# A streaming encoder step on one Trainium2 core: sample attention with its components combined ahead of the transposes, split V, and split squares in the norm

## Chip, cores and metric

The kernel runs on one core of one Trainium2 chip. The metric is the device time of one execution in microseconds (us). Before the change it is the median of three runs. A profile of one further execution gives the spans of the engines: TensorE (PE), VectorE (DVE), ScalarE (ACT), GpSimd (POOL), and SyncE (SP), which issues every DMA of this kernel.

## The reference

One layer of a hybrid encoder, for a new stream of 2048 frames (the prompt) and for 64 next frames of a running stream (the sample) that has 4096 past frames. Everything is fp32. Cut to what matters here:

```python
def diff_attention(q, k, v, q_pos, k_pos, lam, slopes):     # 4 heads, 2 components c of 64, values of 128
    s = jnp.einsum('bqhcd,bkhcd->bhcqk', q, k).astype(jnp.float32) * (DK_A ** -0.5)
    dist = jnp.abs(q_pos[:, None] - k_pos[None, :]).astype(jnp.float32)
    s = s - slopes[None, :, None, None, None] * dist[None, None, None]
    allowed = (k_pos[None, :] // CHUNK) <= (q_pos[:, None] // CHUNK)
    s = jnp.where(allowed[None, None, None], s, -jnp.inf)
    p = jax.nn.softmax(s, axis=-1)
    a = p[:, :, 0] - lam * p[:, :, 1]
    return jnp.einsum('bhqk,bkhe->bqhe', a.astype(v.dtype), v)

def layer_output(x, oa, ob, za, zb, ga, gb, subln_g, lam_init, w_oa, w_ob, w_out):
    oa = (rmsnorm(oa, subln_g) * (1.0 - lam_init)).reshape(B, T, W_A) * jax.nn.silu(za)
    ob = rmsnorm(ob).reshape(B, T, W_B) * jax.nn.silu(zb)
    m = ga * (oa @ w_oa) + gb * (ob @ w_ob)
    return x + m @ w_out
...
        h = rmsnorm(x, norm_g) @ w_in      # 6144 columns: q, k, v, z of attention and retention, gates
        k_all = jnp.concatenate([cache_k_diff[l].astype(ka.dtype), ka], axis=1)
        v_all = jnp.concatenate([cache_v_diff[l].astype(va.dtype), va], axis=1)
        oa = diff_attn_step(qa, k_all, v_all, past, lam, slopes)
```

The sample's attention is thus 64 queries against 4096 + 64 keys in 4 heads with 2 components. The second branch (retention, per chunk of 64 frames) is computed beside it.

## The kernel before, in words

**Order.** The instruction order of PE, ACT and DVE is written out by a planner inside the kernel. Each piece of work is a Python generator with a priority. The planner keeps a model clock for each engine (`P`, `A`, `V`, `G`, lines 119 to 133; `ld` for DMAs, which are modelled as bytes at 300 per ns plus 2600 ns). At each step `loop` runs the generator of best priority whose wake time has come on PE's model clock; a generator yields the time at which its next input should be there. Buffers are counted with `take` and `give`. On the chip every engine runs its instructions in that order and waits on semaphores; SP's DMA queue is in order too.

**Streams.** The w stream (priority 9, the last) multiplies the normalised x with w_in, in two halves of 1024 frames, the first with the sample's 64 frames. Its matmuls are L500; operands are split into a high and a low fp32r part, three products each. Weights are loaded into three staging buffers ("ws"), cast by ACT (L462), subtracted by POOL (L472), and kept in twelve buffers. Results are taken out of PSUM (tag "mm", two buffers) by ACT (L770) or by the finishing routines, and stored to scratch in DRAM. The z stream (priority 4) runs, half by half, the prompt's attention (`qk_block`, `softmax`, `at_pv`), in the first half also the sample's attention and retention, and the prompt's retention (`ret_block`, matmuls L1301 and on). The second half's attention waits until the w stream has made that half's q, k and v. When both streams have ended, the out stream (L1556 on) applies the output projections.

**Sample attention** (`sample_attn`, L1080). Queries of both components stand on the 128 rows: component 0 in rows 0..63, component 1 in rows 64..127. For a head, eight blocks of 512 cached keys and one of 64 new ones are loaded (`s_loader`, tag K), split into two fp32r parts (ACT L1146, DVE L1148), multiplied (L1111 to L1113), and taken out with the position bias by DVE (L1121) into four row buffers of 128 x 1024 and a tail of 64. ACT exponentiates (L1168, L1173) and sums. `sample_pv` (L1209) then runs in nine steps: four transposes (L1242) of 128 x 128, a copy out of PSUM by ACT (L1256) or DVE (L1253) into "ath" or "atl", and four fp32 matmuls (L1228) with P as the stationary and V as the moving operand, 128 columns. Rows of both components go through the transposes and the matmuls. The result is scaled by row with 1/sum or -lambda/sum (L1266), and after four heads a matmul with `fold` (L1181) adds the two row halves.

**Norm of the attention output** (`rms_t`, L794). With the features on the partitions, the mean of squares is a matmul of a constant 1/128 matrix with the squares. It runs 32 times for the prompt (4 heads, 8 pairs of blocks) and once for the sample:

```python
        nc.scalar.activation(sq, ps, AF.Square)
        t1 = self.A(n, t)
        nc.scalar.copy(o, ps)
        t2 = self.A(n, t)
        self.give(tag, t2)
        yield t1
        yield from self.take("tp")
        mb = self.psum("tp")[:, :n]
        nc.tensor.matmul(mb, self.ones, sq, start=True, stop=True)
```

**Buffers.** `ROWS` = 8 row buffers of 4 KB a partition; K and V have four buffers each.

Of the kernel before, what the change touches and what calls it, by code (L numbers as in the profile page):

```python
# [60 lines left out]
class Hybrid:  # L61
# [732 lines left out]
    def rms_t(self, ps, n, gain, t, tag, tmp=None):  # L794
        nc = self.nc
        if tmp is None:
            for k in ("r_o", "r_sq", "r_y"):
                yield from self.take(k)
            tmp = [self.sb(self.tp_, [128, 256], k)[:, :n] for k in ("r_o", "r_sq", "r_y")]
            own = True  # L800
        else:
            own = False
        o, sq, y = tmp
        nc.scalar.activation(sq, ps, AF.Square)
# [7 lines left out]
        nc.tensor.matmul(mb, self.ones, sq, start=True, stop=True)  # L812
# [9 lines left out]
        nc.vector.scalar_tensor_tensor(out=sq, in0=mb, scalar=EPS, in1=sq, op0=ALU.add, op1=ALU.mult)  # L822
# [257 lines left out]
    def sample_attn(self):  # L1080
        nc = self.nc
# [8 lines left out]
        for h in range(4):  # L1090
# [84 lines left out]
            self.spawn(self.sample_pv(h, units, tail, te, lp, oall), 2, "z")  # L1175
        yield lambda: self.n_spv == 4
# [12 lines left out]

    def s_loader(self):  # L1190
        for h in range(4):
            for m in range(8):
# [15 lines left out]

    def sample_pv(self, h, units, tail, te, lp, oall):  # L1209
        nc = self.nc  # L1210
        ap, sp = self.ap, self.sp
        yield te[-1]
        w = sp.tile([128, 1], F32, tag="s_w", name="s_w", bufs=3)
        nc.vector.tensor_reduce(w, lp[:, :9], axis=AX.X, op=ALU.add)
        nc.vector.reciprocal(w, w)
        nc.vector.tensor_mul(w, w, self.lsam)
        for _ in range(3):
            tw = self.V(9)
        yield from self.take("pv")
        pv = self.psum("pv")[:, :128]  # L1220
        done = [0.0]

        def mms(m, nt, r, a, tag, t):
            yield lambda: len(self.vcs) > 0
            vc, t2 = self.vcs.pop(0)
            yield max(t, t2)
            for k in range(nt):
                nc.tensor.matmul(pv, a[:r, 128 * k:128 * k + 128], vc[:r, k, :],  # L1228
                                 start=m == 0 and k == 0, stop=m == 8)
                done[0] = self.P(512)  # L1230
            self.give(tag, done[0])
            self.give("V", done[0])
            yield self.pe

        todo = None
        for m in range(9):
            nt, r = (4, 128) if m < 8 else (1, 64)
            yield from self.take("at")
            at = self.psum("at")
            for k in range(nt):  # L1240
                src = units[m // 2][:, (m % 2) * 512 + 128 * k:(m % 2) * 512 + 128 * k + 128] if m < 8 else tail
                nc.tensor.transpose(at[:r, 128 * k:128 * k + 128], src, self.ident)  # L1242
                t = self.P(256)
            if m < 8 and m % 2:
                self.give("row", t)
            tag = ("ath", "atl")[m % 2]
            if todo is not None and not self.has(tag):
                yield from mms(*todo)
                todo = None
            yield from self.take(tag)  # L1250
            a = self.sb(ap, [128, 512], tag, "atp")
            if m % 2:
                nc.vector.tensor_copy(a[:r, :128 * nt], at[:r, :128 * nt])  # L1253
                t = self.V(128 * nt, t)
            else:
                nc.scalar.copy(a[:r, :128 * nt], at[:r, :128 * nt])  # L1256
                t = self.A(128 * nt, t)
            self.give("at", t)
            yield self.pe
            if todo is not None:  # L1260
                yield from mms(*todo)
            todo = (m, nt, r, a, tag, t)
# [4 lines left out]
        self.t_spv = self.V(128, max(t, tw))  # L1267
        self.give("pv", self.t_spv)
        self.n_spv += 1
# [8 lines left out]
    def ret_block(self, k, t0, r, first):  # L1278
# [477 lines left out]
    def run(self):  # L1756
# [19 lines left out]
        with tc.manual_schedule(engines=MANUAL(ET)):  # L1776
            self.ident = self.cp.tile([128, 128], F32, tag="ident", name="ident")
            self.xt_ready = []
            self.ones = self.cp.tile([128, 128], F32, tag="ones", name="ones")
            nc.vector.memset(self.ones, 1.0 / 128.0)  # L1780
# [76 lines left out]
```

## Time and profile before

| | |
|---|---|
| runs shown | 2001.48 us median (2001.47 to 2004.52, three runs) |
| the profiled execution | 2002.83 us |
| its span, first to last instruction | 2001.0 us |
| granted TensorE clock, mean | 0.999 |
| sample QK matmuls (L1111) | 421.7 to 572.5 us |
| sample PV matmuls (L1228) | 460.3 to 595.9 us, 264 instructions |
| norm's matmuls (L812) | 219.8 to 1511.8 us, 66 instructions |

How to read the rows quoted below: an engine's busy time is the union of its instructions' spans. Matmuls are pipelined and their ends are modelled, so the length of one matmul is longer than the distance to the next; where a price is wanted, the distance of starts is used. "PEld" is the weight load, which overlaps matmuls. A row of a group has: line, engine, operation, written tile <- read tiles, shape, xcount, and durations min/median/max in ns or busy us and mean ns. A row of waits has: who waits <- for whom, us in total, times, longest. An fp32 matmul appears as two instructions in the counts, a transpose or an fp32r matmul as one. A row of "busy tenths" divides the span into 40 slices of 50 us.

### The profile page before, as it was taken

What the parts mean: (1) busy time and instruction counts of PE and PEld (TensorE: products, weight loads), DVE (VectorE), ACT (ScalarE), POOL (GpSimd) and SP (SyncE); (2) the same over time, 40 slices, a digit from 0 to 9 for tenths busy, and PEclk for the clock granted to TensorE, in tenths of its full rate; (3) what the DMA queues carried; (4) which work ended last, traced back from release to release, by engine and by line L of the source; (5) the groups of instructions that cost most, each with busy time, mean ns of one, the idle gap of its engine ahead of it and who ended that gap; (6) DMA issues with size and microseconds to landing.
All of it is one profiled execution on the core that took longest, in us unless ns stands there. A gap on an engine that the chain in (4) does not pass through costs nothing.

```text
span 2001.0 us, 34243 instructions
## 1 busy us (share of the span) xinstructions
PE 1985.4 (99%) x12402; PEld 1780.0 (89%) x12402; DVE 992.0 (50%) x2665; ACT 958.6 (48%) x2096; POOL 414.8 (21%) x383
## 2 busy tenths in 40 slices
PE   9999999999999999999999999999999999999999
PEld 7778999999998999999999888888888898889997
DVE  6453666553331421546866555644653457444432
ACT  6432676654442433535766655644654555333330
POOL 2310211211112221221211121221112434222210
PEclk9999999999999999999999999999999999999999
DMA  7646454344565463563353252372233676444431
GB/s 242 202 144 181 131 163 121 105 144 139 158 173 132 136 177 107 160 198 127 110 152 100 75 161 77 106 204 90 74 98 106 203 222 194 152 129 142 135 92 53
DMA packets 330269, 280.96 MB, mean 140 GB/s; under 512 B 64690, under 2 KB 296114, under 8 KB 330099
## 3 DMA queue, kind: packets, MB, share of 16 engines
q1 hardware_dynamic: 330098, 278.77, 47.2%
q8 instruction: 98, 1.61, 0.4%
q14 instruction: 73, 0.59, 0.1%
HBM read 187.19 MB, written 91.49 MB: 139 GB/s over the span
## 4 chain that ended last, share of the span: by engine, by line
PE 95%; DVE 2%; DMA 1%; ACT 1%; issue 0%; SPq 0%; POOL 0%; ACTq 0%; POOLq 0%
PE mm L500 53%; PE s L944 3%; PE s L945 3%; PE at L1624 3%; PE at L1051 3%; PE at L1625 3%; PE at L1626 3%; PE pv L1031 2%; PE pv L1030 2%; PE pv L1029 2%; PE mm L1556 2%; PE mm L1558 2%; PE mm L1557 2%; PE s L1558 2%; PE s L1557 2%; PE s L1556 2%
## 5 line engine op out<-in xcount | busy, mean ns | idle before, releaser
L500 PE MATMUL mm<-xh,wh 128*128 128x512 f32 (+2 forms) x1280 | 461.2, 360 | 0.0
L500 PE MATMUL mm<-xh,wl 128*128 128x512 f32 (+2 forms) x1280 | 451.7, 353 | 0.0
L500 PE MATMUL mm<-xl,wh 128*128 128x512 f32 (+2 forms) x1280 | 450.9, 352 | 0.0
L472 POOL TENSOR_TENSOR wl<-ws,wh 128x512 fp32r<-128x512 f32 x189 | 250.0, 1335 | 906.3 <-ACT wh L462 642.3
L500 PE MATMUL mm<-wh,xh 128*128 128x256 f32 (+3 forms) x864 | 272.1, 315 | 0.5 <-DVE tlo L713 0.3
L500 PEld LDWEIGHTS mm<-xh,wl 128*128 128x128 f32 x1280 | 240.9, 188 | 32.0
L500 PEld LDWEIGHTS mm<-xh,wh 128*128 128x128 f32 x1280 | 241.2, 188 | 29.7 <-issue 0.2
L500 PEld LDWEIGHTS mm<-xl,wh 128*128 128x128 f32 x1280 | 241.4, 189 | 29.0
L500 PE MATMUL mm<-wh,xl 128*128 128x256 f32 (+3 forms) x864 | 266.9, 309 | 0.1
L500 PE MATMUL mm<-wl,xh 128*128 128x256 f32 (+3 forms) x864 | 266.5, 308 | 0.0
L770 ACT COPY ev<-mm 128x512 f32<-128x512 f32 x140 | 71.4, 510 | 241.7 <-PE mm L500 223.1
L500 PEld LDWEIGHTS mm<-wh,xh 128*128 128x128 f32 (+1 forms) x864 | 162.2, 188 | 11.5 <-ACT xh L388 0.6
L500 PEld LDWEIGHTS mm<-wl,xh 128*128 128x128 f32 (+1 forms) x864 | 162.4, 188 | 10.5
L500 PEld LDWEIGHTS mm<-wh,xl 128*128 128x128 f32 (+1 forms) x864 | 162.2, 188 | 10.6 <-DVE xl L389 0.6
L1066 DVE TENSOR_TENSOR atl<-at,ath 128x512 fp32r<-128x512 f32 (+1 forms) x144 | 93.7, 659 | 140.7 <-ACT ath L1064 140.6
L983 ACT ACTIVATE row<-row,a_mx 128x1024 f32<-128x1024 f32 (+7 forms) x160 | 153.5, 963 | 16.6 <-DVE a_mx L963 16.4
L953 DVE CUSTOM_DVE_ANT_0 row<-s,dfar 128x512 f32<-128x512 f32 (+2 forms) x192 | 117.8, 631 | 73.0 <-PE s L945 71.8
L462 ACT CAST wh<-ws 128x512 fp32r<-128x512 f32 x192 | 116.5, 618 | 40.7 <-PE mm L500 28.0
L1064 ACT CAST ath<-at 128x512 fp32r<-128x512 f32 (+1 forms) x144 | 79.5, 563 | 98.9 <-PE at L1051 96.6
L944 PE MATMUL s<-K,q 128*128 128x512 f32 (+3 forms) x320 | 120.2, 381 | 2.5 <-DVE a_acc L953 2.5
L945 PE MATMUL s<-K,q 128*128 128x512 f32 (+3 forms) x320 | 115.4, 362 | 0.0
L1004 DVE SCALAR_TENSOR_TENSOR row<-row,a_w 128x1024 f32<-128x1024 f32 (+4 forms) x96 | 98.1, 1031 | 26.7 <-ACT row L1001 26.5
(207 smaller groups left out, 3943.6 us busy)
## 6 DMA issues: line engine op xcount, KB each, us to landing
ws<-in_w_in_dram SPq DMA_DIRECT2D x192, 256.0 KB, 3.1
q<-qT SPq DMA_DIRECT2D x128, 128.0 KB, 3.0
V<-vN SPq DMA_DIRECT2D x24, 512.0 KB, 5.1
K<-kT SPq DMA_DIRECT2D x48, 256.0 KB, 4.3
gt<-gaT SPq DMA_DIRECT2D x64, 132.0 KB, 2.1
gt<-gbT SPq DMA_DIRECT2D x64, 132.0 KB, 2.2
xt<-in_x_prompt_dram SPq DMA_DIRECT2D x16, 512.0 KB, 6.0
kn<-in_cache_k_T_dram SPq DMA_DIRECT2D x32, 256.0 KB, 4.0
```

What stands on the lines that cost most here:

```text
L462: self.nc.scalar.copy(h, st)
L472: self.nc.gpsimd.tensor_sub(l, st, h.bitcast(F32))
L500: nc.tensor.matmul(ps, p, q, start=c == 0 and i == 0, stop=c == KC - 1 and i == 2)
L944: nc.tensor.matmul(ps, q1s, kk, start=True, stop=False)
L945: nc.tensor.matmul(ps, q2s, kk, start=False, stop=True)
L953: nc.vector.tensor_tensor_reduce(out=units[k0 // 1024][:, k0 % 1024:k0 % 1024 + n], in0=ps, in1=tab, scale=-SLOPES[h], scalar=3.0e38, op0= ...
L983: nc.scalar.activation(u, u, AF.Exp, bias=mx, scale=-1.0, accum_out=lp[:, k:k + 1])
L1004: nc.vector.scalar_tensor_tensor(out=u0, in0=u0, scalar=w[:, 0:1], in1=u1, op0=ALU.mult, op1=ALU.add)
L1066: nc.vector.tensor_sub(al[:, :w], at[:, :w], ah[:, :w].bitcast(F32))
L1556: nc.tensor.matmul(ps, wh[:, csl], oh, start=kt == 0, stop=False)
L1557: nc.tensor.matmul(ps, wh[:, csl], ol, start=False, stop=False)
L1558: nc.tensor.matmul(ps, wl[:, csl], oh, start=False, stop=kt == 3)
```

## The change

In the sample's attention the two components are combined ahead of the transposes. For each head, the sums of the two row halves are exchanged by two small DMAs, and the exponentials are copied between partition halves: `both[k]` receives in its lower half rows the second component of key half 0 and in its upper half the first component of key half 1. DVE then forms p0 - lambda (l0/l1) p1 in place, so that one row buffer holds 64 queries for 1024 keys of key half 0 (rows 0..63) and 1024 keys of key half 1 (rows 64..127). A transpose of 128 x 128 gives 64 queries for two blocks of 128 keys. Out of PSUM each block is split into its high and low fp32r part, which stand side by side as a stationary operand of 64 + 64 columns. V is split by a new task `v_split` (ACT copy, DVE subtraction) into high and low parts side by side, a moving operand of 256 columns; V is now staged in the K buffers, and the V buffers hold the split. The four products land in one 128 x 256 PSUM tile, whose column halves are added with the scale 1/l0 by ACT and DVE. The new keys' tail is handled on 64 rows.

In `rms_t` the output is copied first, the squares are taken from the copy twice, once in fp32 and once in fp32r, DVE subtracts them, and two fp32r matmuls take the place of the fp32 one. `ROWS` goes from 8 to 10, `r_hi` and `r_lo` are new buffers, `ret_block` takes its row buffer before its PSUM tile, the ones matrix is an fp32r tile, and the descriptor scratch is set to 1024 bytes a partition.

```diff
-ROWS = 8
+ROWS = 10
-        "ws": 3, "w": 12, "r_o": 1, "r_sq": 1, "r_y": 1, "state": 2,
+        "ws": 3, "w": 12, "r_o": 1, "r_sq": 1, "r_y": 1, "r_hi": 1, "r_lo": 1, "state": 2,
@@ rms_t
-        nc.scalar.activation(sq, ps, AF.Square)
-        t1 = self.A(n, t)
+        for k in ("r_hi", "r_lo"):
+            yield from self.take(k)
+        hi, lo = (self.sb(self.tp_, [128, 256], k, None, F32R)[:, :n] for k in ("r_hi", "r_lo"))
         nc.scalar.copy(o, ps)
         t2 = self.A(n, t)
         self.give(tag, t2)
+        nc.scalar.activation(sq, o, AF.Square)
+        self.A(n, t)
+        nc.scalar.activation(hi, o, AF.Square)
+        t1 = self.A(n, t)
         yield t1
+        nc.vector.tensor_sub(lo, sq, hi.bitcast(F32))
+        t = self.V(n, t1)
+        yield t
         yield from self.take("tp")
         mb = self.psum("tp")[:, :n]
-        nc.tensor.matmul(mb, self.ones, sq, start=True, stop=True)
-        t = self.P(4 * n)
+        nc.tensor.matmul(mb, self.ones_r, hi, start=True, stop=False)
+        nc.tensor.matmul(mb, self.ones_r, lo, start=False, stop=True)
+        self.P(n)
+        t = self.P(n)
@@ sample_attn
-            yield from self.take("row", 4)
+            yield from self.take("row", 6)
             units = [self.row() for _ in range(4)]
+            both = [self.row("both") for _ in range(2)]
@@ s_loader
-            for m in range(9):
-                yield from self.take("V")
-                vc = self.sb(self.ap, [128, 4, 128], "V", "vc")
+            for m in (0, 4, 1, 5, 2, 6, 3, 7, 8):
+                yield from self.take("K")
+                vc = self.sb(self.ap, [128, 4, 128], "K", "vc")
+    def v_split(self):
+        nc = self.nc
+        for m in 4 * [*range(9)]:
+            nt, r = (4, 128) if m < 8 else (1, 64)
+            yield lambda: len(self.vcs) > 0
+            vc, t = self.vcs.pop(0)
+            yield from self.take("V")
+            yield t + 600
+            v = self.sb(self.ap, [128, 4, 2, 128], "V", "vhl", F32R)
+            c, h, l = vc[:r, :nt], v[:r, :nt, 0], v[:r, :nt, 1]
+            nc.scalar.copy(h, c)
+            t = self.A(128 * nt, self.pe)
+            yield t
+            nc.vector.tensor_sub(l, c, h.bitcast(F32))
+            t = self.V(128 * nt, t)
+            self.give("K", t)
+            self.vhl.append((v, t))
@@ sample_pv
-        nc.vector.tensor_reduce(w, lp[:, :9], axis=AX.X, op=ALU.add)
-        nc.vector.reciprocal(w, w)
-        nc.vector.tensor_mul(w, w, self.lsam)
+        nc.vector.tensor_reduce(l, lp[:, :9], axis=AX.X, op=ALU.add)
+        nc.vector.tensor_copy(num[lo], l[lo])
+        nc.vector.tensor_copy(den[up], l[up])
...
+        self.ld(num[up], l[lo], 1 << 12)
+        t = self.ld(den[lo], l[up], 1 << 12)
+        tt = sp.tile([64, 64], F32, tag="s_tt", name="s_tt", bufs=2)
+        self.ld(tt, tail[up], 1 << 14)
+        for k in range(2):
+            self.ld(both[k][lo], units[k][up], 1 << 18)
+            t = self.ld(both[k][up], units[2 + k][lo], 1 << 18)
+        yield t + 600
+        nc.vector.reciprocal(den, den)
+        nc.vector.scalar_tensor_tensor(out=den, in0=num, scalar=den, in1=self.nlam, op0=ALU.mult, op1=ALU.mult)
+        nc.vector.reciprocal(num, num)
...
+            nc.vector.scalar_tensor_tensor(out=b[lo], in0=b[lo], scalar=den[lo], in1=units[k][lo],
+                                           op0=ALU.mult, op1=ALU.add)
+            nc.vector.scalar_tensor_tensor(out=b[up], in0=units[2 + k][up], scalar=den[up], in1=b[up],
+                                           op0=ALU.mult, op1=ALU.add)
...
+        nc.vector.scalar_tensor_tensor(out=tt, in0=tt, scalar=den[lo], in1=tail[lo], op0=ALU.mult, op1=ALU.add)
...
-                nc.tensor.matmul(pv, a[:r, 128 * k:128 * k + 128], vc[:r, k, :],
-                                 start=m == 0 and k == 0, stop=m == 8)
-                done[0] = self.P(512)
+                    nc.tensor.matmul(pv, a[:r, 128 * k:128 * k + 128], v[:r, k].rearrange("p s e -> p (s e)"),
+                                     start=m == 0 and k == 0 and tag == "ath", stop=m == 4)
+                    done[0] = self.P(256)
...
-                src = units[m // 2][:, (m % 2) * 512 + 128 * k:(m % 2) * 512 + 128 * k + 128] if m < 8 else tail
-                nc.tensor.transpose(at[:r, 128 * k:128 * k + 128], src, self.ident)
+                src = both[m // 2][:, (m % 2) * 512 + 128 * k:(m % 2) * 512 + 128 * k + 128] if m < 4 else tt
+                nc.tensor.transpose(at[:r, r * k:r * k + r], src, self.ident[:r, :r])
...
+                c = at[:r, :128 * nt].rearrange("p (k c q) -> p k c q", c=2, q=64)[:, :, k]
+                s = a[:r, :128 * nt].rearrange("p (k c q) -> p k c q", c=2, q=64)
+                nc.scalar.copy(s[:, :, 0], c)
+                nc.vector.tensor_sub(s[:, :, 1], c, s[:, :, 0].bitcast(F32))
...
-        nc.vector.tensor_scalar_mul(oall[:, 128 * h:128 * h + 128], pv, w)
+        nc.scalar.activation(oh, pv[:, 0:128], AF.Identity, scale=num)
+        nc.vector.scalar_tensor_tensor(out=oh, in0=pv[:, 128:256], scalar=num, in1=oh, op0=ALU.mult, op1=ALU.add)
@@ ret_block
+        yield from self.take("row")
+        ru = self.row("rru")
         yield from self.take("pv")
...
-        yield from self.take("row")
-        ru = self.row("rru")
@@ kernel
-    nc = _bacc.Bacc("TRN2", target_bir_lowering=False, num_devices=1)
+    nc = _bacc.Bacc("TRN2", target_bir_lowering=False, num_devices=1, dynamic_dma_scratch_size=1024)
```

The planner's waits, the model's times and the buffer bookkeeping of these pieces change with them and are left out here.

More of the change, by code (lines that the diff above doesn't have):

```diff
@@ new lines, in sample_pv @@
+        nc.vector.scalar_tensor_tensor(out=den, in0=num, scalar=den, in1=self.nlam, op0=ALU.mult, op1=ALU.mult)
+        nc.vector.reciprocal(num, num)
+        for _ in range(3):
+            self.V(1, t)
+        tb = []
+        for k in range(2):
+            b = both[k]
+            nc.vector.scalar_tensor_tensor(out=b[lo], in0=b[lo], scalar=den[lo], in1=units[k][lo],
+                                           op0=ALU.mult, op1=ALU.add)
+            self.V(1024)
+            nc.vector.scalar_tensor_tensor(out=b[up], in0=units[2 + k][up], scalar=den[up], in1=b[up],
+                                           op0=ALU.mult, op1=ALU.add)
+            tb.append(self.V(1024))
+            self.give("row", tb[-1], 2)
+            yield self.pe
@@ L1219, in sample_pv, with mms @@
+        nc.vector.scalar_tensor_tensor(out=tt, in0=tt, scalar=den[lo], in1=tail[lo], op0=ALU.mult, op1=ALU.add)
+        tb.append(self.V(64))
         yield from self.take("pv")
-        pv = self.psum("pv")[:, :128]
+        pv = self.psum("pv")[:, :256]
         done = [0.0]
[L1223 to L1228, printed above, removed]
-                                 start=m == 0 and k == 0, stop=m == 8)
-                done[0] = self.P(512)
-            self.give(tag, done[0])
-            self.give("V", done[0])
-            yield self.pe
+        def mms(m, nt, r, parts):
+            for a, tag, t in parts:
+                yield lambda: len(self.vhl) > 0
+                v, t2 = self.vhl.pop(0)
+                yield max(t, t2)
+                for k in range(nt):
+                    nc.tensor.matmul(pv, a[:r, 128 * k:128 * k + 128], v[:r, k].rearrange("p s e -> p (s e)"),
+                                     start=m == 0 and k == 0 and tag == "ath", stop=m == 4)
+                    done[0] = self.P(256)
+                self.give(tag, done[0])
+                self.give("V", done[0])
+                yield self.pe
@@ L1235, in sample_pv @@
         todo = None
-        for m in range(9):
-            nt, r = (4, 128) if m < 8 else (1, 64)
+        for m in range(5):
+            nt, r = (4, 128) if m < 4 else (1, 64)
+            yield tb[m // 2]
             yield from self.take("at")
@@ L1240, in sample_pv @@
             for k in range(nt):
-                src = units[m // 2][:, (m % 2) * 512 + 128 * k:(m % 2) * 512 + 128 * k + 128] if m < 8 else tail
-                nc.tensor.transpose(at[:r, 128 * k:128 * k + 128], src, self.ident)
+                src = both[m // 2][:, (m % 2) * 512 + 128 * k:(m % 2) * 512 + 128 * k + 128] if m < 4 else tt
+                nc.tensor.transpose(at[:r, r * k:r * k + r], src, self.ident[:r, :r])
                 t = self.P(256)
-            if m < 8 and m % 2:
+            if m == 1 or m == 3:
                 self.give("row", t)
-            tag = ("ath", "atl")[m % 2]
-            if todo is not None and not self.has(tag):
+            tags = ("ath", "atl") if m < 4 else ("ath",)
+            if todo is not None and not self.has(*tags):
                 yield from mms(*todo)
                 todo = None
[L1250 to L1258, printed above, removed]
+            parts = []
+            for k, tag in enumerate(tags):
+                yield from self.take(tag)
+                a = self.sb(ap, [128, 512], tag, "atp", F32R)
+                c = at[:r, :128 * nt].rearrange("p (k c q) -> p k c q", c=2, q=64)[:, :, k]
+                s = a[:r, :128 * nt].rearrange("p (k c q) -> p k c q", c=2, q=64)
+                nc.scalar.copy(s[:, :, 0], c)
+                t2 = self.A(64 * nt, t)
+                nc.vector.tensor_sub(s[:, :, 1], c, s[:, :, 0].bitcast(F32))
+                t2 = self.V(64 * nt, t2)
+                parts.append((a, tag, t2))
+            self.give("at", t2)
             yield self.pe
@@ L1261, in sample_pv @@
                 yield from mms(*todo)
-            todo = (m, nt, r, a, tag, t)
+            todo = (m, nt, r, parts)
         yield from mms(*todo)
@@ L1778, in run @@
             self.xt_ready = []
-            self.ones = self.cp.tile([128, 128], F32, tag="ones", name="ones")
+            self.ones_r = self.cp.tile([128, 128], F32R, tag="ones", name="ones")
+            self.ones = self.ones_r.bitcast(F32)
             nc.vector.memset(self.ones, 1.0 / 128.0)
```

19 lines of the change are left out of this document (14 added, 5 removed).

## The prediction, made before the change was run

> **What bounds the kernel now.** I read the page first: busy time by engine and the chain that ended last.
>
> ```profile
> span 2001.0 us, 34243 instructions
> PE 1985.4 (99%) x12402; PEld 1780.0 (89%) x12402; DVE 992.0 (50%) x2665; ACT 958.6 (48%) x2096; POOL 414.8 (21%) x383
> PE 95%; DVE 2%; DMA 1%; ACT 1%; issue 0%; SPq 0%; POOL 0%; ACTq 0%; POOLq 0%
> ```
>
> PE lies on 95% of the chain; DVE and ACT are half idle. That is a mean over stages, so next come the windows (span; then busy time and count of PE, PEld, DVE, ACT, POOL; granted clock, DMA share, GB/s), among them the two that hold the sample attention, and PE's waits.
>
> ```profile
> 20.00:1980.00 1960.00, 1952.20 (x12265) 1756.52 (x12264) 976.48 (x2636) 945.75 (x2070) 406.90 (x373) 1.00 0.48 139
> 1980.00:2001.00 21.00, 16.86 (x73) 10.57 (x71) 2.75 (x4) 0.00 (x0) 0.00 (x0) 1.00 0.17 51
> ```
> ```profile
> 400.00:500.00 100.00, 100.00 (x639) 91.20 (x638) 44.76 (x125) 49.91 (x115) 15.88 (x14) 1.00 0.49 142
> 500.00:600.00 100.00, 98.93 (x681) 91.54 (x680) 38.15 (x105) 40.19 (x92) 11.97 (x9) 1.00 0.60 165
> ```
> ```profile
> PE mm L557 <- ACT wh L462: 2.1, 2, 1.4
> PE s L1111 <- DMA ath<-kT: 1.1, 1, 1.1
> ```
>
> Between the opening and the last 21 us PE is idle for 7.8 us of 1960, at granted clock 1.00, and no stage is bound by anything else. While the sample attention waits for something, PE has projection matmuls (L500) to run. So the time is the sum of what PE executes: a microsecond of PE work removed is a microsecond gained, and anything else costs only what it leaves PE idle.
>
> **PE work removed and added, sample attention.** Busy times of matmuls overlap, so I price them by the distance of their starts, in the PE timeline (start, length, what).
>
> ```profile
> 458.04 1.03 PE L1242 MATMUL at<-ident,row 128*128 128x128 f32 x8
> 458.83 0.36 PE L500 MATMUL mm<-xh,wh 128*128 128x256 f32 x1
> 459.03 0.28 PE L500 MATMUL mm<-xl,wh 128*128 128x256 f32 x1
> ...
> 460.23 0.28 PE L500 MATMUL mm<-xh,wl 128*128 128x256 f32 x1
> ...
> 461.23 0.60 PE L1242 MATMUL at<-ident,row 128*128 128x128 f32 x4
> 461.67 1.06 PE L1228 MATMUL pv<-vc,atp 128*128 128x128 f32 x8
> 462.56 0.60 PE L1242 MATMUL at<-ident,row 128*128 128x128 f32 x4
> ...
> 467.88 0.60 PE L1242 MATMUL at<-ident,row 128*128 128x128 f32 x4
> ```
>
> One round is four transposes and four fp32 matmuls, each matmul two passes (x8). Five rounds, 461.23 to 467.88, take 6.65 us: 1.33 each, of which 0.44 is the transposes (0.11 each; the eight at 458.04 give 0.79/8 = 0.10) and 0.89 the matmuls (0.222 each). A head has eight rounds and a tail of one transpose and one matmul: 8 x 1.33 + 0.33 = 10.97 us.
>
> After: the two softmax components are subtracted before the transposes, so 16 transposes and one 64x64 remain: 17 x 0.11 = 1.87. The matmuls become 34 in fp32r with 256 moving columns (V's high and low part). That form stands in the timeline: ten intervals from 459.03 to 460.23, 0.12 each, the weight load hidden. 34 x 0.12 = 4.08. A head costs 5.95, saving 5.02; four heads **20.1 us** (19 to 21 with 0.10 for a transpose and 0.115 to 0.125 for a matmul).
>
> **The norm.** rms_t runs 33 times (L812 x66 are 33 pairs).
>
> ```profile
> 219.82 0.59 PE L812 MATMUL tp<-r_sq,ones 128*128 128x256 f32 x2
> 220.06 0.58 PE L944 MATMUL s<-K,q 128*128 128x512 f32 x1
> 220.48 0.40 PE L945 MATMUL s<-K,q 128*128 128x512 f32 x1
> 220.72 0.28 PE L944 MATMUL s<-K,q 128*128 128x256 f32 x1
> ```
> ```profile
> L812 PE MATMUL tp<-r_sq,ones x66: 377/378/382, 219.8 to 1511.8; 128*128 128x256 f32 x66
> L804 ACT ACTIVATE r_sq<-pv x33: 361/384/392, 219.0 to 1510.4; 128x256 f32<-128x256 f32 x33
> ...
> L822 DVE SCALAR_TENSOR_TENSOR r_sq<-tp,r_sq x33: 359/415/425, 226.1 to 1516.4; 128x256 f32<-128x256 f32 x33
> ```
>
> From 219.82 to 220.72 PE does the pair and two 512-column matmuls of 0.24 (220.48 to 220.72); the pair takes 0.90 - 0.48 = 0.42. Two fp32r matmuls of 256 columns take 0.24. 33 x 0.18 = **5.9 us** saved. The QK part, the fold and all projections keep their instructions.
>
> **What ACT and DVE get.** Nearest rows:
>
> ```profile
> L1146 ACT CAST ath<-kn x32: 617/623/643, 418.3 to 565.2; 128x512 fp32r<-128x512 f32 x32
> L1148 DVE TENSOR_TENSOR atl<-kn,ath x32: 681/692/1821, 419.1 to 566.4; 128x512 fp32r<-128x512 f32 x32
> ```
> ```profile
> L1256 ACT COPY atp<-at x20: 258/587/587, 458.8 to 594.2; 128x512 f32<-128x512 f32 x16, 64x128 f32<-64x128 f32 x4
> L1253 DVE COPY atp<-at x16: 690/691/692, 459.1 to 593.1; 128x512 f32<-128x512 f32 x16
> ```
> ```profile
> L1004 DVE SCALAR_TENSOR_TENSOR row<-row,a_w 128x1024 f32<-128x1024 f32 (+4 forms) x96 | 98.1, 1031 | 26.7 <-ACT row L1001 26.5
> ```
>
> Per head: V split, 8 x 0.62 + 0.26 on ACT and 8 x 0.69 + 0.3 on DVE (5.2 and 5.8); the subtraction of the components, 4 x 1.03 and about seven small operations on DVE (5); P split by 256-column halves, 8 x 0.38 on ACT and 8 x 0.42 on DVE (3.0 and 3.4). Gone are 4 x 0.59 + 0.26 on ACT and 4 x 0.69 on DVE. Net about 5.6 us ACT and 11.4 us DVE a head; four heads raise ACT from 90 to 113 and DVE from 83 to 129 us of the 200 between 400 and 600. The norm adds one ACT and one DVE operation of 0.4 us, 13 us each over the run. Cost taken: nothing; the cover is the projections, which need no DVE in this stage (L770, a copy on ACT, empties their PSUM). Without that cover DVE's 46 us would stand on the path.
>
> POOL's subtraction for the weights runs beside these two-operand DVE operations, and the 692 ns operation has been seen at 1821 ns. POOL is busy 28 of the 200 us, so some 14% of 57 new operations may lose up to 1.13 us, 9 us of DVE time at most, inside DVE's idle 71. [...]
>
> **Later heads, rows, queues.** The chain inside a head grows (copies, subtraction, V waiting in K's four buffers). What z work is late next is retention (L1301), then the second half's attention.
>
> ```profile
> L944 PE MATMUL s<-K,q x320: 218/393/583, 206.3 to 1476.6; 128*128 128x512 f32 x88, 128*128 128x256 f32 x40, 128*128 128x384 f32 x24, 128*128 128x128 f32 x8
> ...
> busy tenths in 40 slices 0000322200000000002213212201310000000000
> ```
>
> L944, the QK matmul of the prompt, rests in slices 8 to 17, 400 to 900 us; the last evacuation of sample P (L1256 and L1253 above, to 594) lies well before. Even 50 us more in the sample stage meets no deadline, and ROWS 10 instead of 8 loosens it. The smaller descriptor scratch I cost at nothing: of 330269 packets the page gives 330098 to the hardware queue, the rest to instruction fetch. Taking ret_block's row before its PSUM tile adds no instruction.
>
> **The copies between partition halves.** Nothing like them is in the trace. Seven go out per head (four of 256 KB, three small) on SP's queue; DVE's reciprocal then waits, and behind it in DVE's order stand the next head's QK evacuations (L1121), which PE waits for. The nearest rows are the stores of r_o, 128 KB out of SBUF:
>
> ```profile
> L136 SPq DMA_DIRECT2D oaT<-r_o x36: 314/342/857, 231.0 to 1523.4; - x36
> ...
> DMA to landing us min/median/max: 1.7/1.8/4.2
> ```
>
> Issue 0.31 to 0.86 us each, landing 1.7 to 4.2: 7 x 0.31 + 1.7 = 3.9 to 7 x 0.86 + 4.2 = 10.2 us. The planner allows 4 x 0.874 + 0.07 + 2.6 + 0.6 = 6.8 before it emits the waiting instruction. So DVE is 2.9 early to 3.4 late per head, and PE loses 0 to 14 us in all. The medians (0.34, 1.8) are near the lower end, but SP and the queues also carry the loads of this stage: I take 0.5 per head, **2 us**. The loads behind the copies on SP come up to 6 us later; the weights among them have three staging and twelve split buffers, and PE's only wait for a weight is L557's, in the opening. V's split makes ACT wait for a load, with L770 behind it; PE waited for no such load before, and the plan leaves 0.6 us: inside the range.
>
> **Sum.** The profiled execution took 2002.83 us (span 2001.0 and 1.8 around it), 1.35 above the median of the runs shown. 2002.83 - 20.1 - 5.9 + 2 = 1978.8; against the median, **1977 us**. What no-change looks like for this kernel is 0.2%, 4 us.
>
> **Rivals.** The first leans on the L1111 row above, the second on a row of SP's own waits (total, times, longest).
>
> ```profile
> SPq L136 <- ACT ev L770: 257.0, 83, 16.0
> ```
>
> 1. *The copies land late* (12%). At 2 to 3.4 us of PE idle per head, 8 to 14 in place of 2: 1983 to 1989. For it: one of the four unprefetched key tails already cost PE 1.1 us. Against: the other three cost none. [...]
> 2. *Slower: DVE blocked in order* (5%). The same wait, prolonged: if SP is held by a store that waits for ACT, the copies issue late, and everything behind the reciprocal stops. It decides from 26/4 = 6.5 us of PE idle per head; at 8 us, half of that longest wait, the time is 2001.5 - 26 + 32 = 2007. For it: SP waited up to 16 us for one L770. Against: such waits follow the plan, and PE, whose projections go on meanwhile, stands still only when it meets a dependent instruction.
> 3. *The new PV matmuls, two 64-column parts side by side, cost what the fp32 ones do* (2%): 34 x 0.222 against 33 x 0.222 leaves 16 transposes less 0.2 a head, 1.5 us, 6 in all; with the norm and the 2 us, 2001.5 - 6 - 6 + 2 = 1991.5. Against: the 0.12 of L500's 256-column form.
> 4. *The reordering also closes idle time* (6%): 7.8 us of PE idle outside opening and end; half of it and no new wait: 1971.
>
> **How the numbers follow.** Forecast 75%, 1972 to 1982 by its own bounds; rivals 12, 5, 2, 6%. The range 1970 to 1988 takes in rival 4 and nearly all of rival 1, and leaves out rival 2 and, by 3 us, rival 3. Faster: 75 + 12 + 2 + 6 less a little of rival 1's tail, 0.93; within 0.2%: 0.02; slower: 0.05.
>
> **What would show it.** PE busy near 1959; 136 PV matmuls 0.12 apart, 68 transposes, ones matmuls near 0.28 long instead of 0.38; DVE near 1050 and ACT near 995 without new PE waits. The forecast is wrong if PE shows idle of microseconds between 400 and 650 with DVE behind a DMA, or if the new matmuls stand over 0.15 apart.

## The result, and the profile after

The changed kernel takes 1989.59 us (median of six runs, 1986.06 to 1991.51) against 2003.67 us of the kernel before, run in turn with it six times: ratio 0.9930, 95% interval 0.9920 to 0.9941, a gain of 14 us. Forecast were 1977 us and a gain of 24; the time lies 1.6 us above the range. The profiled execution took 1990.07 us, 12.8 less than the one before.

The page of the changed kernel, the same three lines as before, and then its window between opening and end:

```profile
span 1988.3 us, 34106 instructions
...
PE 1963.8 (99%) x12206; PEld 1754.7 (88%) x12206; DVE 1057.2 (53%) x2786; ACT 991.0 (50%) x2185; POOL 417.3 (21%) x383
...
PE 64%; DVE 2%; DMA 2%; ACT 1%; issue 0%; POOL 0%; SPq 0%; POOLq 0%; ACTq 0%; DVEq 0%
```
```profile
20.00:1968.00 1948.00, 1931.44 (x12068) 1732.91 (x12067) 1041.70 (x2757) 977.47 (x2158) 409.39 (x373) 1.00 0.49 143
```

PE has 196 instructions less, and DVE and ACT grew as forecast (1057 and 991 us; 1050 and 995 were named). But PE's idle time in this window is 16.6 us of 1948, where it was 7.8. (The chain of this profile adds up to only 69% of the span, where that of before came to 99%, so its 64% for PE can't be set beside the 95% of before.)

The PE timeline of the changed kernel shows the new matmuls:

```profile
502.34 1.12 PE L1294 MATMUL pv<-vhl,atp 128*128 128x256 f32 x8
503.30 0.60 PE L1309 MATMUL at<-ident,both 128*128 128x128 f32 x4
503.65 1.20 PE L1294 MATMUL pv<-vhl,atp 128*128 128x256 f32 x8
504.69 0.60 PE L1309 MATMUL at<-ident,both 128*128 128x128 f32 x4
```

Eight of them take 0.96 and 1.04 us, 0.12 and 0.13 each. Taking each run of such instructions from the start before it to the second start after it, less the usual distance of its neighbours, and summing over all of them, the sample's transposes and PV matmuls cost PE 45.4 us before and 26.3 after (19.1 saved), the norm's matmuls 14.3 and 7.9 (6.4 saved). PE was given 25.5 us less to do; 26.0 were forecast. So half of the gain, 12.7 us of the profiled pair, was lost again. PE's idle time over the whole span grew by 8.9 us, from 15.6 (2001.0 less 1985.4) to 24.5 (1988.3 less 1963.8). The other 3.9 us lie in its busy time, which fell by 21.6 and not by 25.5; a stretch at half clock, below, accounts for 1.7 of them, and where the rest lies was not followed. Who was waited for (PE's waits of the changed kernel; total, times, longest):

```profile
PE tp L1452 <- DVE rru L1446: 4.4, 3, 1.6
PE s L956 <- DVE a_acc L965: 4.2, 6, 1.5
PE mm L500 <- ACT ev L770: 2.8, 2, 2.2
PE mm L557 <- ACT wh L462: 2.0, 2, 1.3
PE tp L667 <- ACT wh L462: 1.9, 1, 1.9
...
PE tp L667 <- DVE raw L652: 0.9, 1, 0.9
```

and the waits on DVE in the same list of the kernel before, whose L944 is L956 of the changed kernel:

```profile
PE s L944 <- DVE a_acc L953: 2.5, 4, 1.6
PE tp L667 <- DVE raw L652: 2.1, 5, 0.9
```

L1452 is a transpose of the retention and L956 a QK matmul of the prompt's attention: instructions that the change leaves as they were. L667 transposes results of the w stream. Neither DMAs between partition halves nor the new PV matmuls appear. The copies themselves (tile `both`, and what DVE waited for in the tile `s_den`):

```profile
L136 SPq DMA_DIRECT2D both<-row x16: 461/546/603, 484.8 to 656.6; - x16
...
DMA to landing us min/median/max: 3.0/3.5/4.1
```
```profile
  DMA s_den<-s_l: 12.4, 4
```

They land in 3.0 to 4.1 us, within the bounds set, and the first of them go out while the exponentials still run. From the first issue to the last landing the four of a head take 7.6 to 9.7 us. DVE stood 3.1 us a head for the small copy of the sums, and no wait of PE follows from it.

Two of the waits can be followed in the timeline. First the retention at 745 us (all engines; the number in brackets is the idle time before):

```profile
740.90 1.30 POOL L1370 TENSOR_TENSOR rvx<-rqk,rtab 128x512 f32<-128x512 f32 x1
741.03 1.19 DVE L233 SCALAR_TENSOR_TENSOR sm_t<-sm_y 128x4 f32<-128x4 f32 x1 [2.36 <-ACT sm_y L230]
742.15 2.54 POOL L472 TENSOR_TENSOR wl<-ws,wh 128x512 fp32r<-128x512 f32 x2
742.26 1.22 DVE L234 TENSOR_TENSOR sm_t<-sm_t,ms 128x4 f32<-128x4 f32 x1
743.51 1.20 DVE L235 SCALAR_TENSOR_TENSOR sm_y<-sm_t,sm_y 128x4 f32<-128x4 f32 x1
744.75 0.69 DVE L1446 TENSOR_TENSOR rru<-rru,sm_y 128x512 f32<-128x512 f32 x1
745.58 0.63 PE L1452 MATMUL tp<-ident,rru 128*128 128x128 f32 x4 [1.28 <-DVE rru L1446]
```

Three DVE operations on four columns, whose lines have medians of 0.164 to 0.166 us, take 1.2 us each: every one ends just behind a POOL instruction, and the next POOL instruction starts before the next DVE operation does. The chain comes 3.1 us late, and PE, in order, waits 1.3 us. Before the waits at 807, 983, 1215, 1249 and 1514 us the same sight: small DVE operations, whose lines have medians of 0.15 to 0.17 us, take 0.7 to 1.3 us beside POOL's subtraction of weights (L472, 1.3 us) or its other products (0.7 and 1.3 us). (The row that names L462 for L667, at 983 us, is taken as such a case. DVE's `raw` ended 0.15 us before the transposes began, where 0.14 lie between DVE's end and PE's start at 745; ACT's instruction ended only 0.04 before.) In this trace 130 DVE operations take over 0.1 us more than the median of their line and form, and POOL was running at the start of every one of them. One such case the prediction had seen in the trace of before (1.821 us for 0.692), and, in its sum, costed at nothing.

The second is in the sample stage, at 490 us:

```profile
482.26 0.71 ACT L1186 ACTIVATE row<-row,s_mx 128x512 f32<-128x512 f32 x1
...
487.92 0.60 ACT L1235 CAST vhl<-vc 128x512 fp32r<-128x512 f32 x1
...
489.69 0.35 ACT L770 COPY ev<-mm 128x256 f32<-128x256 f32 x1
```
```profile
490.10 0.50 PE L500 MATMUL mm<-xh,wh 128*128 128x512 f32 x1 [2.24 <-ACT ev L770]
```

ACT runs a head's eight exponentials, then V's cast and three operations of the norm, and only then the copy that frees the projections' PSUM; both PSUM buffers are full and PE stands 2.2 us.

One wait seems to have cost twice. Before 982.70 PE stood 1.9 us, and from 983.6 to 987.0 us its 256-column matmuls start 0.21 us apart instead of 0.12: 3.4 us at half the granted clock (0.51 in the window from 983.6 to 987.0; below, windows of 4 us, in which the clock is the third number from the end):

```profile
980.00:984.00 4.00, 2.12 (x17) 1.95 (x17) 3.73 (x8) 3.29 (x7) 3.07 (x3) 0.95 0.43 129
984.00:988.00 4.00, 4.00 (x25) 4.00 (x24) 3.88 (x6) 4.00 (x9) 0.02 (x1) 0.62 0.69 222
```

The longer wait of 2.2 us at 490 us was not followed by such a stretch: the clock is 1.00 in the windows from 490 to 498 us. What decides it these traces don't show.

### The profile page after: what moved, and what is told of

The parts are those of the page before. It is cut to its first block, busy times and chain, and to the rows that moved or that the text cites. A ratio compares the mean times of both kernels' runs of the same rounds, so it can differ in the third digit from the quotient of the medians.

```text
span 1988.3 us, 34106 instructions
## 1 busy us (share of the span) xinstructions
PE 1963.8 (99%) x12206; PEld 1754.7 (88%) x12206; DVE 1057.2 (53%) x2786; ACT 991.0 (50%) x2185; POOL 417.3 (21%) x383
## 4 chain that ended last, share of the span: by engine, by line
PE 64%; DVE 2%; DMA 2%; ACT 1%; issue 0%; POOL 0%; SPq 0%; POOLq 0%; ACTq 0%; DVEq 0%
PE mm L500 31%; PE at L1698 3%; PE at L1699 3%; PE at L1700 3%; PE s L956 2%; PE s L957 2%; PE at L1063 2%; PE mm L1630 2%; PE s L1632 2%; PE mm L1631 2%; PE mm L1632 2%; PE s L1631 2%; PE s L1630 2%; PE pv L1043 1%; PE pv L1042 1%; PE pv L1041 1%
## 5 line engine op out<-in xcount | busy, mean ns | idle before, releaser
L500 PE MATMUL mm<-xh,wh 128*128 128x512 f32 (+2 forms) x1280 | 459.3, 359 | 2.8 <-ACT ev L770 2.8
L500 PE MATMUL mm<-xh,wl 128*128 128x512 f32 (+2 forms) x1280 | 452.4, 353 | 0.0
L500 PE MATMUL mm<-xl,wh 128*128 128x512 f32 (+2 forms) x1280 | 451.8, 353 | 0.0
L472 POOL TENSOR_TENSOR wl<-ws,wh 128x512 fp32r<-128x512 f32 x189 | 258.6, 1381 | 867.2 <-ACT wh L462 605.5
L500 PE MATMUL mm<-wh,xh 128*128 128x256 f32 (+3 forms) x864 | 273.5, 317 | 0.3 <-DVE tlo L713 0.3
L500 PEld LDWEIGHTS mm<-xh,wh 128*128 128x128 f32 x1280 | 241.4, 189 | 32.4 <-ACT ev L770 3.3
L500 PEld LDWEIGHTS mm<-xh,wl 128*128 128x128 f32 x1280 | 241.1, 188 | 31.9 <-POOL wl L472 0.4
L500 PE MATMUL mm<-wh,xl 128*128 128x256 f32 (+3 forms) x864 | 267.9, 310 | 0.1
L500 PE MATMUL mm<-wl,xh 128*128 128x256 f32 (+3 forms) x864 | 267.6, 310 | 0.0
L500 PEld LDWEIGHTS mm<-xl,wh 128*128 128x128 f32 x1280 | 241.6, 189 | 27.8
L500 PEld LDWEIGHTS mm<-wh,xh 128*128 128x128 f32 (+1 forms) x864 | 162.8, 188 | 11.8 <-PE s L957 0.4
L500 PEld LDWEIGHTS mm<-wl,xh 128*128 128x128 f32 (+1 forms) x864 | 162.9, 189 | 11.0
L500 PEld LDWEIGHTS mm<-wh,xl 128*128 128x128 f32 (+1 forms) x864 | 162.8, 188 | 10.9 <-DVE xl L389 0.6
L462 ACT CAST wh<-ws 128x512 fp32r<-128x512 f32 x192 | 115.4, 618 | 33.2 <-PE mm L500 22.0
L956 PE MATMUL s<-K,q 128*128 128x512 f32 (+3 forms) x320 | 118.3, 374 | 4.2 <-DVE a_acc L965 4.2
L1016 DVE SCALAR_TENSOR_TENSOR row<-row,a_w 128x1024 f32<-128x1024 f32 (+4 forms) x96 | 102.6, 1074 | 21.5 <-ACT row L1013 21.4
```

What stands on the lines that cost most here:

```text
L462: self.nc.scalar.copy(h, st)
L472: self.nc.gpsimd.tensor_sub(l, st, h.bitcast(F32))
L500: nc.tensor.matmul(ps, p, q, start=c == 0 and i == 0, stop=c == KC - 1 and i == 2)
L956: nc.tensor.matmul(ps, q1s, kk, start=True, stop=False)
L1016: nc.vector.scalar_tensor_tensor(out=u0, in0=u0, scalar=w[:, 0:1], in1=u1, op0=ALU.mult, op1=ALU.add)
```

## The experiments

Eighteen kernels. Theories: W, the loss is waits in the sample stage behind ACT's exponentials; N and later C, the norm's longer chain and added operations cost it; L, collisions of DVE with POOL cost it; O, each instruction order has its own accidents; M, P and S are explained where they are expected. Ratios are against the kernel before measured beside each, whose medians lie between 2001.28 and 2002.44 us, with 95% intervals.

**The parts alone.**

`norm_only`: the kernel before with `rms_t` of the change and the smaller scratch; `pv_only`: the changed kernel with `rms_t` of before; `rows_only`: the kernel before with the smaller scratch and

```diff
-ROWS = 8
+ROWS = 10
...
+        yield from self.take("row")
+        ru = self.row("rru")
         yield from self.take("pv")
...
```

> The kernel before with only the norm's split squares (and the smaller descriptor scratch, which makes room). In the profiles the norm's 33 matmul pairs cost PE 14.3 us before and 7.9 after. Theory W (PE work is saved as priced, and the change's loss is new waits of PE in the sample stage, where ACT runs eight exponentials in a row and the projections' PSUM copy comes late): the norm keeps nearly all of its 6.4 us, 2003.7 - 6.4 = 1997, within 2. Rival N (the longer chain of the norm, one more operation each on ACT and DVE, makes the prompt's attention late and costs the waits seen at 253, 1215 and 1249 us): 2000 or more. Rival O (each instruction order has its own accidental waits, some microseconds either way): anywhere from 1993 to 2003.

> The changed kernel with the norm as before; the sample's new attention, ten rows and the row order stay. Its PE work is 19.1 us less than before (45.4 to 26.3 in the profiles). Theory W: the whole loss of about 11 us sits here: 2003.7 - 19.1 + 11 = 1996. Rival N: the loss goes with the norm: 1985 to 1987. Rival O: anywhere between, with waits at other places than in the changed kernel.

> The kernel before with ten row buffers for eight, the smaller descriptor scratch, and the retention's row taken ahead of its PSUM tile; every instruction is the same, only their order moves. Theory W and rival N: no change, 2003.7 within 2. Rival O: a change of 4 us or more to either side (the planner's own PE clock ends 8.7 us later in this order).

Measured: norm alone 2000.86, ratio 0.9994 (0.9985 to 1.0003); sample's part alone 1983.40, 0.9906 (0.9892 to 0.9919); rows 2004.02, 1.0006 (0.9998 to 1.0015). The sample's part gains 19, all of its PE work; the norm keeps 1 of 6.4, within its interval of nothing. So in this order the loss comes with the norm: W falls as the main cause, N stands for now. Rows and scratch alone don't explain it.

**Room between the exponentials.** `spread1` is the changed kernel, `pv_spread` the sample's part alone, each with

```diff
                 te.append(self.A(512, t, 220))
+                if m < 7:
+                    yield te[-1] - 250
```

> The changed kernel with one edit in the sample's attention: after each of a head's eight exponentials but the last the planner may place other work on ACT, so that the PSUM copies of the projections no longer queue behind all eight. No work is added or removed. Theory W: the waits of 2.4 us at 490 and 0.7 us at 599 and what follows from them go: 1982 to 1985 (the planner's own PE clock ends 14.5 us earlier). Rival N: no change, 1989.6 within 2. Rival O: some microseconds either way, and the waits stand elsewhere.

> The sample's part alone, with other work of ACT allowed between a head's exponentials. Theory W for the two waits of 0.7 us at 514 and 623: 1980 to 1983. Rival O: 1981 to 1988.

Measured: 1985.56, ratio 0.9914 (0.9900 to 0.9928); and 1983.81, 0.9912 (0.9898 to 0.9925). In the first the wait at 490 is gone from the trace and the time is 3 to 4 us lower, 0.6 above W's range; the second gains nothing, as rival O had it. The edit also moves the order, new waits of 5.4 us stand in the output projections, and the interval overlaps that of the changed kernel (0.9920 to 0.9941). So W is at most a part of the loss, the smaller one.

**POOL's subtraction in four pieces.** The planner is told nothing, so PE, ACT and DVE keep their order:

```diff
-            self.nc.gpsimd.tensor_sub(l, st, h.bitcast(F32))
+            k = l.shape[-1] // 4
+            for j in range(4):
+                s = (slice(None),) * (len(l.shape) - 1) + (slice(k * j, k * j + k),)
+                self.nc.gpsimd.tensor_sub(l[s], st[s], h[s].bitcast(F32))
```

> The changed kernel, with POOL's subtraction for the projection weights (L472, 1.29 us) issued in four pieces of 128 columns. PE, ACT and DVE keep their order, and the planner is told nothing. So far: the sample's part alone gained 19.0 us, all of its PE work; the norm alone gained 1.6 of its 6.4, and on top of the sample's part it cost 6.2. Theory L: the waits of PE come from small DVE operations of 0.16 us that stand for 1.0 to 1.3 us while a POOL subtraction runs (745, 807, 983, 1215, 1249, 1514 us in the profile of the changed kernel); the planner does not know of it, and the norm's tight chains make it reach PE. With pieces of some 0.4 us such a stand is short: 1978 to 1983. Rival O: the waits are those of this order of instructions whatever POOL does: 1989.6 within 2. Rival M: POOL's pieces cost more than the whole (four starts) and the weights come late: over 1991.

> The same cut of POOL's subtraction in the kernel with the sample's part alone (1983.4 uncut). Its profile shows few waits of PE (6.1 us in waits over 0.3 us). Theory L: little to gain, 1980 to 1984, so that the norm's 6.4 us come back as a gain when both are cut (the changed kernel cut lies 3 to 6 us below this one). Rival O: 1983.4, and the changed kernel cut stays 6 us above. Rival M: over 1985.

> The same cut in the kernel before (2002.4). Its waits of PE over 0.3 us are 9.0 us in all, 5 of them on DVE. Theory L: 1998 to 2001. Rival O: 2002.4 within 1. Rival M: over 2004.

Measured: changed kernel cut 1988.70, ratio 0.9932 (0.9919 to 0.9946); sample's part cut 1988.90, 0.9931 (0.9918 to 0.9943); kernel before cut 2009.45, 1.0036 (1.0024 to 1.0048). PE's waits of the changed kernel cut (its lines are 3 further: L503 is L500, L475 is L472, L959 is L956, L670 is L667):

```profile
PE mm L503 <- POOL wl L475: 4.9, 3, 3.3
PE mm L503 <- ACT ev L773: 2.8, 2, 2.2
PE mm L560 <- POOL wl L475: 2.0, 1, 2.0
...
PE s L959 <- DVE a_acc L968: 0.8, 3, 0.3
...
PE tp L670 <- DVE raw L655: 0.2, 1, 0.2
```
```profile
L475 POOL TENSOR_TENSOR wl<-ws,wh 128x128 fp32r<-128x128 f32 x756 | 361.1, 513 | 788.2 <-ACT wh L462 555.2 <-PE mm L503 125.8 <-PE s L960 47.7
```

The order is the same, instruction by instruction, on PE and on DVE, and the waits on DVE are all but gone: the retention's from 4.4 us to none, the attention's from 4.2 to 0.8, those of L667 from 2.8 to 0.2. Matched one by one, the seven waits at 253, 745, 807, 983, 1215, 1249 and 1514 us, 9.6 us in all, come to 0.2. PE isn't merely late there for another reason: the nearest new wait of PE ahead of one of the seven is 0.5 us long and stands 32 us before it. That shows the collisions as the cause of those waits. The 2.8 us behind ACT stay. The time is no test of it, since a piece costs 0.51 us, four of them 2.05 for the 1.38 of the whole, and the weights now come late (6.9 us of waits on POOL): the cut alone costs the kernel before 7 and the sample's part 5 us, the changed kernel nothing. Against those two controls the changed kernel won 7 and 5 us by the ratios, each uncertain by some 3 to 4 us. L's times came out nowhere; the changed kernel's 1988.70 is what rival O had named, and rival M was right of the two others.

**The norm's parts.** `norm_ops` is the changed kernel with PE's saving taken away (`self.ones, sq`, one fp32 matmul, for the fp32r pair) and the added operations kept; `norm_hi` is the sample's part alone with one fp32r matmul of squares rounded straight out of PSUM. It leaves out the low part of the squares.

> The changed kernel with the norm's fp32 matmul back, fed by the fp32 squares; the copy first, the two squares, DVE's subtraction and the planner's waits for them stay. PE work as in the sample's part alone (1983.4), ACT and DVE work as in the changed kernel (1989.6). Theory C (the norm's added operations and longer chain cost the microseconds that the fp32r matmuls save): 1989 to 1996. Rival O (the loss is an accident of one order, through collisions of DVE with POOL): 1983.4 within 4, no more likely above than below.

> The sample's part alone, with the norm's squares rounded to fp32r, straight out of PSUM as before, and one fp32r matmul: the low part of the squares is left out, so ACT and DVE do what they did before, and PE's norm work falls from 14.3 to about 4 us. Theory C: all of it is gained, 1983.4 - 10 = 1973, within 2. Rival O: the new order costs something of its own, 1975 to 1984.

Measured: 1987.08, ratio 0.9932 (0.9918 to 0.9946); and 1976.91, 0.9879 (0.9865 to 0.9892). The operations without their gain cost 5 us by the ratios; the gain without the operations brings 5.4 of 10, by the ratios. Theory C gets neither number. Both lie within rival O's wide ranges, the first by 0.3 us.

**Other orders.** The planner's assumed latency decides nothing but the order (260 is shown; 240 is set likewise):

```diff
-LAT = 250.0
+LAT = 260.0
```

> The changed kernel with the planner's assumed latency 260 ns for 250: no work changes, only the order. Theory L (collisions fall where the order puts them): the time moves by some microseconds, 1982 to 1992, and the long waits stand at other places, again with small DVE operations beside POOL's subtraction. Rival P (the norm's longer chain is late at the same places in any order): 1989.6 within 1.5, with the waits at the same places.

> The sample's part alone with the planner's latency 260 ns for 250; only the order moves. If 1983.4 was a lucky order (rival O), it comes out at 1985 to 1989; theory C: 1983.4 within 2. The changed kernel went from 1989.6 to 1986.4 by the same edit.

> The kernel before with the planner's latency 240 ns for 250; the work is the same, the order moves. At 260 ns the sample's part alone went from 1983.4 to 1989.9 and the changed kernel from 1989.6 to 1986.4. If the kernel before stands in a lucky order too (rival S), it comes out at 2005 or more; if its order is an ordinary one, within 3 of 2002.

> The kernel before at 260 ns. Rival S: 2005 or more here too. With the changed kernel at the same 260 ns (1986.4) it gives a second pair: theory O expects pairs that scatter by some 5 us about one mean gain; if the change's loss of about 11 us is its own, each pair shows 11 to 17 us of gain, never the priced 25.

> The changed kernel at 240 ns, the pair of the run of the kernel before at 240. Theory O: 1984 to 1992. The mean of its three orders is then the better measure of the change.

> The sample's part alone at 240 ns: third order of it, after 1983.4 and 1989.9. Theory O: 1983 to 1992, so that the norm on top gains or loses some microseconds by the order, with a mean between 0 and the 6.4 us of PE work. Theory C (the norm's added operations cost): 1983 to 1985, below the changed kernel at 240.

> The norm's added operations with the fp32 matmul (PE work as in the sample's part alone), at 240 ns. At 250 ns it lay 3.7 above the sample's part alone. Theory C (the added operations of ACT and DVE cost in any order): 3 to 6 above the sample's part at 240, 1987 to 1990. Theory O: 1980 to 1988, above or below 1983.8.

> The same at 260 ns, beside the sample's part at 260 (1989.9). Theory C: 1993 to 1996. Theory O: 1984 to 1992.

Medians in us and ratios with their intervals:

| latency | before | sample's part | sample's part, norm's operations | changed kernel |
|---|---|---|---|---|
| 240 | 2004.52, 1.0015 (1.0006 to 1.0024) | 1983.79, 0.9910 (0.9897 to 0.9924) | 1990.79, 0.9942 (0.9930 to 0.9954) | 1981.01, 0.9897 (0.9883 to 0.9910) |
| 250 | the reference, 1 | 1983.40, 0.9906 | 1987.08, 0.9932 | 1989.59, 0.9930 |
| 260 | 2002.95, 1.0005 (0.9996 to 1.0013) | 1989.88, 0.9945 (0.9932 to 0.9957) | 1989.74, 0.9943 (0.9929 to 0.9957) | 1986.38, 0.9918 (0.9904 to 0.9931) |
| mean ratio | 1.0007 | 0.9920 | 0.9939 | 0.9915 |

By the ratios, 0.001 being 2 us: the change gains 23.6, 14.0 and 17.4 us at the three latencies, 18.3 in the mean. At 240 ns nearly all of the 25.5 us of PE work comes through, so the loss does not belong to the change in every order. The norm on top of the sample's part gains 2.6, loses 4.8, gains 5.4, so the verdict on the norm turns with ten nanoseconds of a planner's constant: rival O is shown. (At 250 and 260 ns the intervals of the two kernels just miss each other; at 240 they overlap.) The norm's operations alone cost 6.4, 5.2 and -0.4. Whether they have a price of their own (3.7 in the mean) under a scatter of this size, three orders don't settle. The scatter was wider than rival O's ranges: three of its times missed (1981.01, 1989.88 and 1990.79, by 0.9 to 3 us). The kernel before moves least, by 3 and 1 us; that it stands in a lucky order (rival S) is not shown. The changed kernel at 240 ns beats both kernels, with all of the computation.

The traces bear this out in part. PE's waits on DVE at the retention's transposes, the prompt's QK matmuls and L667, with the row that names ACT, sum to 5.4, 11.4 and 6.4 us in the changed kernel at 240, 250 and 260 ns, and to 1.9, 2.1 and 6.3 us in the sample's part: the slowest order of each has the most of them. They are not the whole of a difference: at 240 and 260 ns the changed kernel's sums are 1 us apart and its times 4 us by the ratios. Nor do all of them move. At 260 ns the retention's three are gone, but those at 253, 983, 1215 and 1249 us are found again within 2 us of the same time, the first in two pieces of 0.5 and 0.4 us. Rival P, which expected the same places, was right of these four and wrong of the time.

## Why the prediction was wrong

**What bounds, and the PE sum: right.** PE is busy for 98.8 to 99.4% of the span in every kernel here, and the terms came out nearly as priced: 19.1 for 20.1 in the sample, 6.4 for 5.9 in the norm. PE's busy time is 1963.8 us where 1959 was named, most of that the 3.9 us told of above.

**"Cost taken: nothing" for ACT and DVE: the step that failed.** The prediction looked for collisions with POOL in the sample stage only, set 9 us of them against 71 us of DVE's idle time there, and called them covered. In that stage this nearly held: between 400 and 700 us PE waits only the 2.8 us behind ACT's eight exponentials with V's cast and the norm behind them, and the sample's part alone kept all of its 19 us in two orders of three. What it put at nothing was the collisions everywhere else, in the prompt's attention, the retention and L667's transposes. DVE's idle time is a mean over a stage; a wait of PE arose where a chain of small operations had to be done by the time the planner gave PE's next instruction to it (at 745 us three of them came 3.1 us late and PE stood 1.3). The sum of stretch on DVE grew only from 77 us to 88 (every DVE operation over 0.1 us longer than the median of its line and form, 126 of them before and 130 after). What changed more is where it fell: DVE's waits in PE's list went from 4.6 us (the L944 and L667 rows of before) to 9.5 (L1452, L956 and L667) and, with the L667 row that names ACT, 11.4; 9.6 of these come down to 0.2 when POOL's instruction is cut. What the norm's added operations cost in it stays open.

**What comes later was taken to stand still.** "Even 50 us more in the sample stage meets no deadline" held: PE has no wait of over 0.1 us between 600 and 745 us. But the planner lays every later instruction anew, so retention, prompt attention and the weights' subtraction met each other at other times. The forecast had no term for that, and its bounds came only from the copies: 0 to 14 us at one place. One latency step moved the sample's part by 6.5 us in the medians (7.8 by the ratios), two thirds of the 10 us between the forecast's own bounds.

**The copies.** The 2 us taken for them were not needed: they land inside the bounds and PE waits for none. Rival 1 gave 1983 to 1989, next to the measured time, for a reason that did not occur: that it came close is luck. The sign that the prediction had set for being wrong, idle of PE with DVE behind a DMA, did not come either. Rival 2 fell with it, rival 3 with the 0.12 to 0.13 us of the new matmuls, and rival 4 went the other way: idle time grew.

## What to carry to other kernels

In a kernel whose order a planner lays out, price a change in the bounding engine's work exactly, but give its time a scatter from reordering, measured by moving a planner's constant; here a step of 10 ns moved one kernel by 6.5 us and with it decided whether the norm's part gained or lost. Judge a small edit by its mean over a few orders, before and after alike. Work on an engine that is half idle is not free where its instructions stand in a short chain with a due time: look in the trace which other engine's instructions run beside that chain and how long they and the chain's own take there; here operations of 0.16 us took 1.2 beside POOL's of 1.3.

## What was not expected of the hardware

DVE operations of 0.16 us took 1.2 us beside POOL's of 1.3, three in a row from 741.03 to 744.71 us, each begun 0.1 us after an instruction of POOL (740.90 and 741.03, 742.15 and 742.26, 743.41 and 743.51). With POOL's subtraction cut, the seven waits of PE fell from 9.6 to 0.2 us and the run's longest L235 from 1.20 to 0.39 us, while the longest L233 and L234 stayed at 1.25 and 1.21; and 128 columns cost 0.51 us where 512 cost 1.38. A wait of PE of 1.9 us at 983 us was followed by 3.4 us at half the granted clock, in the middle of an otherwise full stretch, while one of 2.2 us at 490 us was not.
